# A decoder block's FFN: gate and up computed with the tokens as the stationary operand, their product turned by TensorE transposes, the half-wide block first

## The chip, the core and the metric

The kernel runs on one core of one Trainium2 chip, as one launch. The metric is device microseconds (us) of that core; lower is better. Before the change the median of three runs is 512.78 us.

## What is computed

The block is a pre-norm decoder layer over 256 tokens and a model width of 1024, all in float32. The change touches only its last stage, a SwiGLU FFN with 2816 hidden columns:

```python
h2 = rmsnorm(x, ffn_norm_g[l])
x = x + (jax.nn.silu(h2 @ w_ffn_gate[l]) * (h2 @ w_ffn_up[l])) @ w_ffn_down[l]
```

Ahead of it stand a normalised input projection, two branches (a gated linear recurrence and a block-sparse attention), their gates and the output projection `w_out`; these are as they were.

## The kernel before

All dense products run in split precision. A float32 value is held as a rounded part `hi` (type fp32r) and the rest `lo`; a product is the sum of three, hi·hi, hi·lo and lo·hi. Weights come from HBM in pieces of 1 MB (`load_w`, line 57): one DMA on SyncE's queue into `wraw`, a copy on ScalarE (ACT) that makes `whi` (line 55), and a subtraction on VectorE (DVE) that makes `wlo` (line 56). Each of the three has three buffers, so a piece's buffers are reused three pieces later. Activations that are to be multiplied get the same split.

There are two forms of a dense product. In `tok_block` and in the way down, 128 tokens are the stationary operand (the 128x128 block loaded into TensorE) and 512 weight columns stream past: three matmuls of 512 columns for each 128 inputs and 128 tokens, the result with tokens on the partitions. In `feat_block` (line 86) 128 weight columns are stationary and the tokens stream: for each 128 inputs and 128 outputs one matmul of `whi` against 512 columns (256 tokens hi and 256 tokens lo side by side, line 99) and one of `wlo` against 256 columns (line 98, line 101 for the first of a bank). The result has features on the partitions and its two halves lie side by side, so `fold` (lines 110, 111) adds them with one ACT copy and one DVE add.

The FFN (lines 558 to 634) turns the normalised x2 with TensorE transposes (line 567) into `x2T`, spreads the token scale r2 over the partitions with two small products (`spread`, line 184), and walks over five groups of 512 hidden columns and a last group of 256. In each group `feat_block` makes gate, then up; the folds, the scale, the SiLU and the product give `zt`, already features by tokens, which is what the way down needs as stationary operand. `hT` is its split. `down` (line 584), one group behind, adds two 128-row pieces of `w_down` at a time into four accumulator banks `acc` with matmuls at lines 596 to 598 and at the end adds to x2 and writes out.

Each engine runs its instructions in one fixed order, made at build time by a list scheduler; an instruction that waits holds up all behind it on its engine. PSUM has eight banks: four called `pw` for the products, two `ph` and two `pa` which become `acc` in the FFN.

Of the kernel before, what the change touches and what calls it, by code (L numbers as in the profile page):

```python
# [7 lines left out]
F32 = mybir.dt.float32  # L8
F32R = mybir.dt.float32r
U32 = mybir.dt.uint32  # L10
AF = mybir.ActivationFunctionType
OP = mybir.AluOpType
AX = mybir.AxisListType

P = 128
S = 256
D = 1024
# [3 lines left out]
NFT = DFF // P  # L21
# [6 lines left out]
def tile_hgrn2_moba_block(ctx: ExitStack, tc: tile.TileContext, xm, xT, vecs, table, onehot,  # L28
                          w_in, w_hg, w_at, w_out, w_gate, w_up, w_down, out):
    nc = tc.nc  # L30
    const = ctx.enter_context(tc.tile_pool(name="const", bufs=1))
    big = ctx.enter_context(tc.tile_pool(name="big", bufs=1))
# [5 lines left out]
    def pw(name="pw"):  # L38
        return psum.tile([P, 512], F32, name=name, tag="pw", bufs=4)

    def ph(name="ph"):
        return psum.tile([P, 512], F32, name=name, tag="ph", bufs=2)

    def pa(name="pa"):
        return psum.tile([P, 512], F32, name=name, tag="pa", bufs=2)
# [8 lines left out]
    def split(src, hi, lo):  # L54
        nc.scalar.copy(hi, src)  # L55
        nc.vector.tensor_sub(lo, src, hi.bitcast(F32))  # L56

    def load_w(src, shape, cut=1):
        raw = wp.tile([P] + shape, F32, name="wraw")
        hi = wp.tile([P] + shape, F32R, name="whi")  # L60
        lo = wp.tile([P] + shape, F32R, name="wlo")
        n = shape[0] // cut
        for i in range(0, shape[0], n):
            nc.sync.dma_start(raw[:, i:i + n, :], src[:, i:i + n, :])
            split(raw[:, i:i + n, :], hi[:, i:i + n, :], lo[:, i:i + n, :])
        return hi, lo
# [19 lines left out]
    def feat_block(w, c0, act, cw=512, parts=(4, 4), cut=1):  # L86
        n = cw // P
        ps = [pw() for _ in range(n)]
        k = 0
        for pn in parts:  # L90
            hi, lo = load_w(w[k * P:(k + pn) * P, c0:c0 + cw].rearrange("(k p) c -> p k c", p=P), [pn, cw], cut)
            for ct in range(n):
                cs = slice(ct * P, (ct + 1) * P)
                for i in range(pn):
                    kt = k + i
                    both = act[kt // 4][:, kt % 4, :, :].rearrange("p m t -> p (m t)")
                    if kt > 0:
                        nc.tensor.matmul(ps[ct][:, 0:S], lo[:, i, cs], part(act, kt, 0), start=False, stop=False)  # L98
                    nc.tensor.matmul(ps[ct], hi[:, i, cs], both, start=(kt == 0), stop=(kt == KT - 1))  # L99
                    if kt == 0:  # L100
                        nc.tensor.matmul(ps[ct][:, 0:S], lo[:, i, cs], part(act, kt, 0), start=False, stop=False)  # L101
            k += pn
        return ps

    def fold(dst, p):
        if len(dst.shape) == 3:
            lo, hi = (p[:, m * S:(m + 1) * S].rearrange("p (b t) -> p b t", b=2) for m in range(2))
        else:
            lo, hi = p[:, 0:S], p[:, S:2 * S]
        nc.scalar.copy(dst, hi)  # L110
        nc.vector.tensor_add(dst, lo, dst)  # L111

    def flat():
        return big.tile([P, 4, S], F32, name="fl", tag="T15")
# [14 lines left out]
    for g, pieces in enumerate(((1, 1, 2), (2, 2))):  # L129
# [4 lines left out]
        for n in pieces:  # L134
            ks = slice(k0, k0 + n)
            xs = slice(4 * g + k0, 4 * g + k0 + n)
# [4 lines left out]
            for kt in range(xs.start, xs.stop):  # L141
# [3 lines left out]
                                               op0=OP.mult, op1=OP.subtract)  # L145
                if kt == xs.start:
                    split(raw[:, ks, :], wh[:, ks, :], wl[:, ks, :])
            for i in range(k0, k0 + n):
                kt = 4 * g + i
                for tb in range(2):  # L150
                    ts = slice(tb * P, (tb + 1) * P)
# [7 lines left out]
    ident = const.tile([P, P], F32, name="ident")  # L159
# [3 lines left out]
    for j in range(7):  # L163
        c = 1 << j
        n = 64 // c
        for tb in range(2):
            m = mask[:, j, tb, :].rearrange("p (n c) -> p n c", c=c)
# [11 lines left out]
    def spread(dst, r):  # L179
        dg = small.tile([P, 2, P], F32, name="dg")  # L180
        bank = ph()
        for tb in range(2):
            nc.vector.tensor_scalar_mul(dg[:, tb, :], ident, r[:, tb:tb + 1])
            nc.tensor.matmul(bank[:, tb * P:(tb + 1) * P], ones, dg[:, tb, :], start=True, stop=True)
        nc.vector.tensor_copy(dst, bank[:, :S])
# [369 lines left out]
            split(g, M[half][:, 2 * j:2 * j + 2, 0, :], M[half][:, 2 * j:2 * j + 2, 1, :])  # L555


    x2T = [big.tile([P, 4, 2, S], F32R, name=f"x2T{i}", tag=("XH", "XL")[i]) for i in range(2)]
    ss2 = small.tile([P, 2, 2], F32, name="ss2")
    for half in range(2):  # L560
        ps = tok_block(w_out, half * 512, M)
        for tb in range(2):
            xs = x2[:, tb, half * 512:(half + 1) * 512]
            nc.vector.tensor_add(xs, xs, ps[tb])
            bank = ph()
            for i in range(4):
                nc.tensor.transpose(bank[:, i * P:(i + 1) * P], xs[:, i * P:(i + 1) * P], ident)
            xg = big.tile([P, 4, P], F32, name="xg", tag=("T12", "T13")[tb])
            nc.vector.tensor_mul(xg, bank.rearrange("p (k t) -> p k t", k=4),
                                 vec[:, 8 + half * 4:12 + half * 4].unsqueeze(2).to_broadcast([P, 4, P]))  # L570
            split(xg, x2T[half][:, :, 0, tb * P:(tb + 1) * P], x2T[half][:, :, 1, tb * P:(tb + 1) * P])
            jk2 = big.tile([P, 512], F32, name="jk2", tag="T15")
            nc.scalar.activation(jk2, xs, AF.Square, accum_out=ss2[:, tb, half:half + 1])
    r2 = small.tile([P, 2], F32, name="r2")
    nc.vector.tensor_add(r2, ss2[:, :, 0], ss2[:, :, 1])
    rinv(r2, r2, D)
    R2 = const.tile([P, S], F32, name="R2")
    spread(R2, r2)
    R2b = R2.unsqueeze(1).to_broadcast([P, 2, S])


    acc = [[None, None], [None, None]]

    def down(f0, nf, act, last):
        for j0 in range(0, nf, 2):
            hi, lo = load_w(w_down[(f0 + j0) * P:(f0 + j0 + 2) * P, :].rearrange("(j p) c -> p j c", p=P), [2, D])
            end = last and j0 + 2 == nf
            for tb in range(2):
                for half in range(2):
                    ts = slice(tb * P, (tb + 1) * P)  # L590
                    cs = slice(half * 512, (half + 1) * 512)
                    for i in range(2):
                        j = j0 + i
                        st = f0 + j == 0
                        en = f0 + j == NFT - 1
                        nc.tensor.matmul(acc[tb][half], act[:, j, 0, ts], hi[:, i, cs], start=st, stop=False)  # L596
                        nc.tensor.matmul(acc[tb][half], act[:, j, 0, ts], lo[:, i, cs], start=False, stop=False)  # L597
                        nc.tensor.matmul(acc[tb][half], act[:, j, 1, ts], hi[:, i, cs], start=False, stop=en)  # L598
                    if end:
                        cut = 2 if tb == 1 and half == 1 else 1  # L600
                        cw = 512 // cut
                        for q in range(cut):
                            xs = x2[:, tb, half * 512 + q * cw:half * 512 + (q + 1) * cw]
                            nc.vector.scalar_tensor_tensor(xs, acc[tb][half][:, q * cw:(q + 1) * cw], r2[:, tb:tb + 1],
                                                           xs, op0=OP.mult, op1=OP.add)
                            nc.sync.dma_start(out[tb * P:(tb + 1) * P, half * 512 + q * cw:half * 512 + (q + 1) * cw],
                                              xs)

    pend = None
    for f0 in range(0, NFT, 4):  # L610
        nf = min(4, NFT - f0)
        pg = feat_block(w_gate, f0 * P, x2T, cw=nf * P)
        zt = big.tile([P, 4, S], F32, name="zt", tag=("T12", "T13")[f0 // 4 % 2])
        for j in range(nf // 2):
            z = zt[:, 2 * j:2 * j + 2, :]
            for i in range(2):
                fold(z[:, i, :], pg[2 * j + i])
            nc.vector.tensor_mul(z, z, R2b)
            nc.scalar.activation(z, z, AF.Silu)
        pu = feat_block(w_up, f0 * P, x2T, cw=nf * P)  # L620
        fl = flat()
        hT = big.tile([P, 4, 2, S], F32R, name="hT", tag=("T5", "T6")[f0 // 4 % 2])
        for j in range(nf // 2):
            js = slice(2 * j, 2 * j + 2)
            for i in range(2 * j, 2 * j + 2):
                fold(fl[:, i, :], pu[i])
            nc.vector.tensor_mul(zt[:, js, :], zt[:, js, :], fl[:, js, :])
            split(zt[:, js, :], hT[:, js, 0, :], hT[:, js, 1, :])
        if pend is not None:
            if pend[0] == 0:  # L630
                acc = [[ph("acc00"), ph("acc01")], [pa("acc10"), pa("acc11")]]
            down(*pend, False)
        pend = (f0, nf, hT)
    down(*pend, True)


def _bucket(n):
# [38 lines left out]
```

## Time and profile before

| | us |
|---|---|
| runs | 512.7, 512.78, 514.68; median 512.78 |
| the profiled execution | 513.5 |
| its span, first to last instruction | 511.4 |
| FFN on TensorE, from its first gate matmul to the end of its last matmul's turn | 322.09 to 507.33, that is 185.24 |
| of that: 352 pairs of gate and up matmuls, 264 matmuls of the way down, 8 transposes, 4 records of `spread` | |

The granted TensorE clock is 1.00 of full speed over the whole span (2.4 GHz, the upper of its two levels). A matmul's recorded duration is longer than the time until the next one starts, since they are pipelined; time from start to start is what a chain costs.

### The profile page before, as it was taken

The numbers are of one execution on the slowest core, as the hardware profiler recorded it, in microseconds if no ns is written. First come the engines' busy times: TensorE is split into PE (matmuls) and PEld (weight loads), VectorE is DVE, ScalarE is ACT, GpSimd is POOL, SyncE is SP. The second block draws the span as 40 slices with busy tenths as digits, with TensorE's granted clock in tenths as the row PEclk, the third lists the DMA queues.
The fourth block names the chain that finished last, engine by engine and source line by source line (L and its number), as shares of the span: only waits on it lengthen the run. The fifth ranks groups of instructions, "written<-read, shape, count | busy, mean of one in ns | idle before, by whom it ended". The sixth has DMA issues, their size and how long they took to land.

```text
span 511.4 us, 6690 instructions
## 1 busy us (share of the span) xinstructions
PE 502.2 (98%) x2674; PEld 427.5 (84%) x2674; DVE 350.9 (69%) x406; ACT 291.8 (57%) x447; POOL 25.4 (5%) x42
## 2 busy tenths in 40 slices
PE   6999999999999999999999999999999999999996
PEld 5878878788888888988888888888888888888885
DVE  4769998977597663297667777767665646657372
ACT  5597538776639644975554464665634535444250
POOL 8002340000000000000000000000000000000000
PEclk9999999999999999999999999999999999999999
DMA  7956955725422743256665456555655565553522
GB/s 234 390 197 182 347 178 168 243 82 166 164 84 82 247 142 106 83 171 242 190 213 173 166 181 229 165 164 172 208 198 164 186 226 165 177 193 86 181 105 82
DMA packets 43806, 91.20 MB, mean 178 GB/s; under 512 B 1880, under 2 KB 4472, under 8 KB 43776
## 3 DMA queue, kind: packets, MB, share of 16 engines
q1 hardware_dynamic: 43040, 88.14, 51.8%
q0 software_dynamic: 736, 2.65, 1.7%
q8 instruction: 21, 0.34, 0.3%
q14 instruction: 9, 0.07, 0.0%
HBM read 89.70 MB, written 1.07 MB: 178 GB/s over the span
## 4 chain that ended last, share of the span: by engine, by line
PE 86%; DVE 6%; ACT 3%; DMA 1%; POOL 1%; issue 1%; SPq 0%; DVEq 0%; POOLq 0%
PE pw L99 30%; PE pw L98 13%; PE pw L83 6%; PE pw L81 6%; PE pw L82 6%; PE acc L598 4%; PE acc L596 4%; PE acc L597 4%; DVE wlo L56 3%; PE ph L320 2%; PE pw L101 2%; ACT whi L55 2%; DMA wraw<-w_in 1%; POOL qk L295 1%; PE pa L437 1%
## 5 line engine op out<-in xcount | busy, mean ns | idle before, releaser
L56 DVE TENSOR_TENSOR wlo<-wraw,whi 128x2048 fp32r<-128x2048 f32 (+2 forms) x88 | 190.8, 2169 | 105.4 <-ACT whi L55 105.0
L55 ACT CAST whi<-wraw 128x2048 fp32r<-128x2048 f32 (+2 forms) x88 | 156.0, 1774 | 104.4 <-issue 29.5
L99 PE MATMUL pw<-x2T,whi 128*128 128x512 f32 x352 | 121.8, 398 | 0.0
L99 PE MATMUL pw<-XT,whi 128*128 128x512 f32 x256 | 89.6, 399 | 0.0
L98 PE MATMUL pw<-x2T,wlo 128*128 128x256 f32 x308 | 86.6, 281 | 0.0
L99 PEld LDWEIGHTS pw<-x2T,whi 128*128 128x128 f32 x352 | 63.5, 188 | 12.3
L98 PE MATMUL pw<-XT,wlo 128*128 128x256 f32 x224 | 62.8, 281 | 0.0
L98 PEld LDWEIGHTS pw<-x2T,wlo 128*128 128x128 f32 x308 | 58.3, 189 | 1.8
L81 PE MATMUL pw<-whi,XT 128*128 128x512 f32 x144 | 56.9, 395 | 0.8 <-DVE Q L111 0.8
L82 PE MATMUL pw<-wlo,XT 128*128 128x512 f32 x144 | 56.8, 394 | 0.0
L83 PE MATMUL pw<-whi,XT 128*128 128x512 f32 x144 | 56.5, 392 | 0.0
L99 PEld LDWEIGHTS pw<-XT,whi 128*128 128x128 f32 x256 | 46.5, 188 | 9.9 <-ACT Fg L110 0.4
L98 PEld LDWEIGHTS pw<-XT,wlo 128*128 128x128 f32 x224 | 42.4, 189 | 1.4
L596 PE MATMUL acc<-whi,hT 128*128 128x512 f32 x88 | 34.3, 390 | 0.0
L598 PE MATMUL acc<-whi,hT 128*128 128x512 f32 x88 | 34.3, 390 | 0.0
L597 PE MATMUL acc<-wlo,hT 128*128 128x512 f32 x88 | 34.3, 389 | 0.0
L81 PEld LDWEIGHTS pw<-whi,XT 128*128 128x128 f32 x144 | 27.1, 188 | 6.5 <-DVE Q L111 1.1
L83 PEld LDWEIGHTS pw<-whi,XT 128*128 128x128 f32 x144 | 27.0, 188 | 5.6
L82 PEld LDWEIGHTS pw<-wlo,XT 128*128 128x128 f32 x144 | 27.1, 188 | 5.5 <-DVE wlo L56 0.3
L110 ACT COPY fl<-pw 128x256 f32<-128x256 f32 x38 | 14.0, 370 | 24.9 <-PE pw L99 24.9
L99 PE MATMUL pw<-aT,whi 128*128 128x512 f32 x64 | 22.3, 397 | 0.0
L99 PE MATMUL pw<-oT,whi 128*128 128x512 f32 x64 | 22.3, 397 | 0.0
(209 smaller groups left out, 708.4 us busy)
## 6 DMA issues: line engine op xcount, KB each, us to landing
wraw<-w_in SPq DMA_DIRECT2D x32, 1024.0 KB, 5.2
wraw<-w_down SPq DMA_DIRECT2D x11, 1024.0 KB, 4.8
wraw<-w_gate SPq DMA_DIRECT2D x10, 1024.0 KB, 5.0
wraw<-w_up SPq DMA_DIRECT2D x10, 1024.0 KB, 5.0
wraw<-w_at SPq DMA_DIRECT2D x4, 1024.0 KB, 4.9
wraw<-w_hg SPq DMA_DIRECT2D x4, 1024.0 KB, 5.0
wraw<-w_out SPq DMA_DIRECT2D x4, 1024.0 KB, 5.0
wraw<-w_in SPq DMA_DIRECT2D x7, 512.0 KB, 8.8
```

The source lines that it names most:

```text
L55: nc.scalar.copy(hi, src)
L56: nc.vector.tensor_sub(lo, src, hi.bitcast(F32))
L81: nc.tensor.matmul(ps[tb], part(act, kt, 0)[:, ts], wh, start=(kt == 0), stop=False)
L82: nc.tensor.matmul(ps[tb], part(act, kt, 0)[:, ts], wl, start=False, stop=False)
L83: nc.tensor.matmul(ps[tb], part(act, kt, 1)[:, ts], wh, start=False, stop=(kt == KT - 1))
L98: nc.tensor.matmul(ps[ct][:, 0:S], lo[:, i, cs], part(act, kt, 0), start=False, stop=False)
L99: nc.tensor.matmul(ps[ct], hi[:, i, cs], both, start=(kt == 0), stop=(kt == KT - 1))
L101: nc.tensor.matmul(ps[ct][:, 0:S], lo[:, i, cs], part(act, kt, 0), start=False, stop=False)
L110: nc.scalar.copy(dst, hi)
L596: nc.tensor.matmul(acc[tb][half], act[:, j, 0, ts], hi[:, i, cs], start=st, stop=False)
L597: nc.tensor.matmul(acc[tb][half], act[:, j, 0, ts], lo[:, i, cs], start=False, stop=False)
L598: nc.tensor.matmul(acc[tb][half], act[:, j, 1, ts], hi[:, i, cs], start=False, stop=en)
```

## The change

Gate and up are computed in the token form: tokens stationary, 512 weight columns streaming (256 in the half-wide group, which now goes first). `x2T` is stored by 128 tokens (`cb`). The SiLU on ACT reads a bank directly and takes r2 as its per-partition scale, so `fold`, `spread` and the multiplication with R2 are gone; a DVE multiplication with the up bank, also read directly, gives `zt`, tokens by features. For the way down `turn` transposes `zt` on TensorE, a group later, into the banks that up will use next (`bX`, `bZ`), and `split` reads them there and writes `hT`. The way down takes its pieces from a list, `todo`, at fixed places between the gate and up blocks. `pw`'s four banks get fixed roles: `bV`, `bY` gate for the two token halves, `bX`, `bZ` up.

```diff
-    x2T = [big.tile([P, 4, 2, S], F32R, name=f"x2T{i}", tag=("XH", "XL")[i]) for i in range(2)]
+    xq = big.tile([P, 2, 2, 4, P], F32, name="xq", tag="T11")
+    cb = []
+    for tag in ("XH", "XL"):
+        two = big.tile([P, 2, 4, 2, P], F32R, name="cb" + tag, tag=tag)
+        cb += [two[:, 0], two[:, 1]]
+
+    def combine(m, p):
+        split(xq[:, p[0], p[1]], cb[m][:, :, 0, :], cb[m][:, :, 1, :])
...
-    R2 = const.tile([P, S], F32, name="R2")
-    spread(R2, r2)
-    R2b = R2.unsqueeze(1).to_broadcast([P, 2, S])
...
+    acc = [[ph("acc00"), ph("acc01")], [pa("acc10"), pa("acc11")]]
+    bV, bY, bX, bZ = pw("bV"), pw("bY"), pw("bX"), pw("bZ")
+
+    def product(ps, c, hi, lo, first, last):
+        for k in range(4):
+            nc.tensor.matmul(ps, c[:, k, 0, :], hi[:, k, :], start=(first and k == 0), stop=False)
+            nc.tensor.matmul(ps, c[:, k, 0, :], lo[:, k, :], start=False, stop=False)
+            nc.tensor.matmul(ps, c[:, k, 1, :], hi[:, k, :], start=False, stop=(last and k == 3))
...
+        def gate(self, tb, src):
+            nc.scalar.activation(self.z[:, tb], src, AF.Silu, scale=r2[:, tb:tb + 1])
+
+        def turn(self, tb, bank):
+            for j in range(self.nf):
+                nc.tensor.transpose(bank[:, j * P:(j + 1) * P], self.z[:, tb, j * P:(j + 1) * P], ident)
+            src = bank[:, :self.cw].rearrange("p (j t) -> p j t", j=self.nf)
+            ts = slice(tb * P, (tb + 1) * P)
+            split(src, self.hT[:, :self.nf, 0, ts], self.hT[:, :self.nf, 1, ts])
+            if tb == 1:
+                todo.extend((self.hT, self.f, j0) for j0 in range(0, self.nf, 2))
...
+        def block(self, w, banks, kh):
+            hi, lo = load_w(self.quarter(w, kh), [4, self.cw])
             for tb in range(2):
+                product(banks[tb][:, :self.cw], cb[plain[kh][tb]], hi, lo, kh == 0, kh == 1)
+
+        def run(self, prev):
+            self.open()
+            self.block(w_gate, (bV, bY), 0)
+            if prev:
+                down()
+            else:
+                self.block(w_up, (bX, bZ), 0)
+            self.block(w_gate, (bV, bY), 1)
+            for tb in range(2):
+                self.gate(tb, (bV, bY)[tb][:, :self.cw])
+            if prev:
+                prev.turn(0, bX)
+                prev.turn(1, bZ)
+                self.block(w_up, (bX, bZ), 0)
+                down()
+            self.block(w_up, (bX, bZ), 1)
+            self.close()
+            for tb in range(2):
+                nc.vector.tensor_mul(self.z[:, tb], self.z[:, tb], (bX, bZ)[tb][:, :self.cw])
+
+    order = ((5, Eight), (0, Eight), (1, Eight), (2, Eight), (3, Eight), (4, Eight))
...
-        pg = feat_block(w_gate, f0 * P, x2T, cw=nf * P)
...
-            for i in range(2):
-                fold(z[:, i, :], pg[2 * j + i])
-            nc.vector.tensor_mul(z, z, R2b)
-            nc.scalar.activation(z, z, AF.Silu)
-        pu = feat_block(w_up, f0 * P, x2T, cw=nf * P)
...
-            nc.vector.tensor_mul(zt[:, js, :], zt[:, js, :], fl[:, js, :])
-            split(zt[:, js, :], hT[:, js, 0, :], hT[:, js, 1, :])
+    down()
+    prev.turn(0, bV)
+    prev.turn(1, bY)
+    while todo:
+        down()
```

TensorE in the changed kernel, at the place where the fourth group's gate ends (`whi_3240` is its gate piece, `zt_3010` the third group's product, `whi_3314` and `wlo_3315` a piece of `w_down`, `whi_3284` a piece of up):

```order
L596 MATMUL bY_2717<-whi_3240,cbXL_2537 128x512
L645 MATMUL bX_2718<-ident_185,zt_3010 128x128 x4
L645 MATMUL bZ_2719<-ident_185,zt_3010 128x128 x4
L613 MATMUL acc00_2712<-whi_3314,hT_3175 128x512
L614 MATMUL acc00_2712<-wlo_3315,hT_3175 128x512
L613 MATMUL acc01_2713<-whi_3314,hT_3175 128x512
L614 MATMUL acc01_2713<-wlo_3315,hT_3175 128x512
L594 MATMUL bX_2718<-whi_3284,cbXH_2536 128x512
```

Eight transposes and the way down's first four matmuls now stand between gate and up; those four read `hT_3175`, which is made from the transposes just ahead of them. In the kernel before, the same engine passes from the third group's up to the way down of the group ahead of it (`hT_3086`), made during the block in between:

```order
L98 MATMUL pw_3261<-x2T1_2536,wlo_3302 128x256
L99 MATMUL pw_3261<-x2T1_2536,whi_3301 128x512
L596 MATMUL acc00_3101<-whi_3355,hT_3086 128x512
L597 MATMUL acc00_3101<-wlo_3356,hT_3086 128x512
L598 MATMUL acc00_3101<-whi_3355,hT_3086 128x512
```

ACT in the changed kernel at the same place (`bV` and `bY` are the fourth group's gate, `hT_3175` the hi part of the turned product):

```order
L55 CAST whi_3314<-wraw_3313 128x2048
L641 ACTIVATE zt_3178<-bV_2716,r2_2707 128x512
L641 ACTIVATE zt_3178<-bY_2717,r2_2707 128x512
L55 CAST hT_3175<-bX_2718 128x4x128
L55 CAST hT_3175<-bZ_2719 128x4x128
L55 CAST whi_3344<-wraw_3343 128x2048
```

The SiLU of both gate banks stands ahead of the copies that TensorE's next matmul reads. In the kernel before, ACT's order around a group's product is this (`fl_3085` up's fold, `hT_3086` its split):

```order
L110 COPY fl_3085<-pw_3008 128x256
L55 CAST whi_3170<-wraw_3169 128x2048
L55 CAST hT_3086<-zt_2992 128x2x256 x2
L55 CAST whi_3208<-wraw_3207 128x2048
```

There the copy into `hT` has a whole block of other matmuls ahead of its reader.

## Rows read from the trace of the kernel before

**Rows 1.** Page, first part: engine, busy us, share of the span, instructions.

```profile
PE 502.2 (98%) x2674; PEld 427.5 (84%) x2674; DVE 350.9 (69%) x406; ACT 291.8 (57%) x447; POOL 25.4 (5%) x42
```

**Rows 2.** TensorE's waits over the whole span: us in total, times, longest.

```profile
PE pw L152 <- ACT whi L55: 2.8, 2, 2.4
...
PE ph L305 <- DVE A L306: 0.2, 1, 0.2
```

**Rows 3.** Busy time by stretch: us, PE, PEld, DVE, ACT, POOL, clock, DMA share, GB/s.

```profile
368.49:379.39 10.90, 10.90 (x49) 9.01 (x48) 7.33 (x7) 5.13 (x5) 0.00 (x0) 1.00 0.58 194
379.39:401.92 22.53, 22.53 (x129) 19.61 (x128) 13.04 (x14) 10.98 (x13) 0.00 (x0) 1.00 0.57 188
490.96:507.33 16.37, 16.37 (x73) 13.34 (x71) 8.16 (x9) 2.81 (x3) 0.00 (x0) 1.00 0.09 33
...
322.09:368.49 46.40, 46.40 (x269) 40.41 (x268) 33.43 (x44) 28.43 (x38) 0.00 (x0) 1.00 0.54 182
```

**Rows 4.** Timeline of TensorE from the way down into gate: start, us, operation.

```profile
378.94 0.39 PE L597 MATMUL acc<-wlo,hT 128*128 128x512 f32 x1
379.17 0.39 PE L598 MATMUL acc<-whi,hT 128*128 128x512 f32 x1
379.39 0.39 PE L99 MATMUL pw<-x2T,whi 128*128 128x512 f32 x1
379.62 0.28 PE L101 MATMUL pw<-x2T,wlo 128*128 128x256 f32 x1
379.73 0.28 PE L98 MATMUL pw<-x2T,wlo 128*128 128x256 f32 x1
379.85 0.40 PE L99 MATMUL pw<-x2T,whi 128*128 128x512 f32 x1
380.08 0.28 PE L98 MATMUL pw<-x2T,wlo 128*128 128x256 f32 x1
```

**Rows 5.** Timeline of TensorE at the FFN's start, four transposes among matmuls.

```profile
322.09 0.39 PE L99 MATMUL pw<-x2T,whi 128*128 128x512 f32 x1
322.36 0.66 PE L567 MATMUL ph<-ident,x 128*128 128x128 f32 x4
322.77 0.36 PE L101 MATMUL pw<-x2T,wlo 128*128 128x256 f32 x1
322.97 0.28 PE L98 MATMUL pw<-x2T,wlo 128*128 128x256 f32 x1
```

**Rows 6.** The transposes of line 567: recorded duration in ns, min/median/max.

```profile
L567 PE MATMUL ph<-ident,x x16: 272/273/328, 310.5 to 323.4; 128*128 128x128 f32 x16
```

**Rows 7.** Timeline of TensorE, a chain of short matmuls in the recurrence.

```profile
153.50 1.95 PE L320 MATMUL ph<-QA,KP 128*128 128x128 f32 x16
155.19 0.48 PE L81 MATMUL pw<-whi,XT 128*128 128x512 f32 x1
```

**Rows 8.** Timeline, a 256-column matmul whose stationary operand came late.

```profile
31.78 2.29 DVE L56 TENSOR_TENSOR wlo<-wraw,whi 128x2048 fp32r<-128x2048 f32 x1 [1.05 <-ACT whi L55]
...
34.13 0.39 PE L101 MATMUL pw<-XT,wlo 128*128 128x256 f32 x1
...
34.35 0.28 PE L98 MATMUL pw<-XT,wlo 128*128 128x256 f32 x1
```

**Rows 9.** Timeline from TensorE over ACT to DVE, attention's values and the SiLU ahead.

```profile
180.91 0.39 PE L83 MATMUL pw<-whi,XT 128*128 128x512 f32 x1
...
181.33 1.37 ACT L509 ACTIVATE sg<-pw,rx 128x512 f32<-128x512 f32 x2 [1.55 <-PE pw L83]
...
183.32 0.58 ACT L55 CAST aT<-pa 128x512 fp32r<-128x512 f32 x1 [0.62 <-PE pa L474]
...
183.94 0.69 DVE L56 TENSOR_TENSOR aT<-pa,aT 128x512 fp32r<-128x512 f32 x1 [3.13 <-ACT aT L55]
```

**Rows 10.** Timeline of ACT, two scaled copies out of PSUM back to back.

```profile
153.07 1.31 ACT L221 ACTIVATE Va<-pw,rx 128x512 f32<-128x512 f32 x2 [0.71 <-PE pw L83]
```

**Rows 11.** The fold copy of line 110, 256 columns out of PSUM: duration in ns.

```profile
L110 ACT COPY zt<-pw x22: 358/372/374, 330.7 to 485.5; 128x256 f32<-128x256 f32 x22
```

**Rows 12.** The SiLU of line 509, read from PSUM: duration in ns.

```profile
L509 ACT ACTIVATE sg<-pw,rx x4: 687/688/688, 181.3 to 200.0; 128x512 f32<-128x512 f32 x4
```

More of the change, by code (lines that the diff above doesn't have):

```diff
@@ L555, in tile_hgrn2_moba_block @@
             split(g, M[half][:, 2 * j:2 * j + 2, 0, :], M[half][:, 2 * j:2 * j + 2, 1, :])
-    x2T = [big.tile([P, 4, 2, S], F32R, name=f"x2T{i}", tag=("XH", "XL")[i]) for i in range(2)]
+    xq = big.tile([P, 2, 2, 4, P], F32, name="xq", tag="T11")
[5 more added lines that the diff above has]
+        split(xq[:, p[0], p[1]], cb[m][:, :, 0, :], cb[m][:, :, 1, :])
+    plain = [[0, 1], [2, 3]]
     ss2 = small.tile([P, 2, 2], F32, name="ss2")
@@ L567, in tile_hgrn2_moba_block @@
                 nc.tensor.transpose(bank[:, i * P:(i + 1) * P], xs[:, i * P:(i + 1) * P], ident)
-            xg = big.tile([P, 4, P], F32, name="xg", tag=("T12", "T13")[tb])
-            nc.vector.tensor_mul(xg, bank.rearrange("p (k t) -> p k t", k=4),
+            nc.vector.tensor_mul(xq[:, half, tb], bank.rearrange("p (k t) -> p k t", k=4),
                                  vec[:, 8 + half * 4:12 + half * 4].unsqueeze(2).to_broadcast([P, 4, P]))
-            split(xg, x2T[half][:, :, 0, tb * P:(tb + 1) * P], x2T[half][:, :, 1, tb * P:(tb + 1) * P])
+            combine(plain[half][tb], (half, tb))
             jk2 = big.tile([P, 512], F32, name="jk2", tag="T15")
@@ L576, in tile_hgrn2_moba_block @@
     rinv(r2, r2, D)
-    R2 = const.tile([P, S], F32, name="R2")
-    spread(R2, r2)
-    R2b = R2.unsqueeze(1).to_broadcast([P, 2, S])
[L582 to L587, printed above, removed]
-            for tb in range(2):
-                for half in range(2):
-                    ts = slice(tb * P, (tb + 1) * P)
-                    cs = slice(half * 512, (half + 1) * 512)
-                    for i in range(2):
[L593 to L607, printed above, removed]
@@ L609, in tile_hgrn2_moba_block @@
-    pend = None
-    for f0 in range(0, NFT, 4):
-        nf = min(4, NFT - f0)
-        pg = feat_block(w_gate, f0 * P, x2T, cw=nf * P)
[L613 to L616, printed above, removed]
-                fold(z[:, i, :], pg[2 * j + i])
-            nc.vector.tensor_mul(z, z, R2b)
-            nc.scalar.activation(z, z, AF.Silu)
-        pu = feat_block(w_up, f0 * P, x2T, cw=nf * P)
[L621 to L626, printed above, removed]
-            nc.vector.tensor_mul(zt[:, js, :], zt[:, js, :], fl[:, js, :])
-            split(zt[:, js, :], hT[:, js, 0, :], hT[:, js, 1, :])
[L629 to L633, printed above, removed]
@@ L634, in tile_hgrn2_moba_block @@
-    down(*pend, True)
+    acc = [[ph("acc00"), ph("acc01")], [pa("acc10"), pa("acc11")]]
+    bV, bY, bX, bZ = pw("bV"), pw("bY"), pw("bX"), pw("bZ")
+    todo = []
+    done = [0]
+    def product(ps, c, hi, lo, first, last):
[3 more added lines that the diff above has]
+            nc.tensor.matmul(ps, c[:, k, 1, :], hi[:, k, :], start=False, stop=(last and k == 3))
@@ new lines, in down @@
+    def down():
+        if not todo:
+            return
+        hT, f, j0 = todo.pop(0)
+        hi, lo = load_w(w_down[(f + j0) * P:(f + j0 + 2) * P, :].rearrange("(j p) c -> p j c", p=P), [2, D])
+        done[0] += 2
+        for tb in range(2):
+            for half in range(2):
+                ts = slice(tb * P, (tb + 1) * P)
+                cs = slice(half * 512, (half + 1) * 512)
+                ac = acc[tb][half]
+                for i in range(2):
+                    j = j0 + i
+                    st = done[0] == 2 and i == 0
+                    en = done[0] == NFT and i == 1
+                    nc.tensor.matmul(ac, hT[:, j, 0, ts], hi[:, i, cs], start=st, stop=False)
+                    nc.tensor.matmul(ac, hT[:, j, 0, ts], lo[:, i, cs], start=False, stop=False)
+                    nc.tensor.matmul(ac, hT[:, j, 1, ts], hi[:, i, cs], start=False, stop=en)
+                if done[0] == NFT:
+                    cut = 2 if tb == 1 and half == 1 else 1
+                    cw = 512 // cut
+                    for q in range(cut):
+                        os = slice(half * 512 + q * cw, half * 512 + (q + 1) * cw)
+                        nc.vector.scalar_tensor_tensor(x2[:, tb, os], ac[:, q * cw:(q + 1) * cw], r2[:, tb:tb + 1],
+                                                       x2[:, tb, os], op0=OP.mult, op1=OP.add)
+                        nc.sync.dma_start(out[ts, os], x2[:, tb, os])
@@ new lines, in tile_hgrn2_moba_block, with __init__, quarter, open @@
+    class Unit:
+        def __init__(self, n, u):
+            self.n, self.f, self.c0 = n, 4 * u, u * 512
+            self.nf = min(4, NFT - 4 * u)
+            self.cw = self.nf * P
+        def quarter(self, w, r):
+            return w[r * 512:(r + 1) * 512, self.c0:self.c0 + self.cw].rearrange("(k p) c -> p k c", p=P)
+        def open(self):
+            self.z = big.tile([P, 2, 512], F32, name="zt", tag=("T12", "T13")[self.n % 2])[:, :, :self.cw]
+        def close(self):
+            self.hT = big.tile([P, 4, 2, S], F32R, name="hT", tag=("T6", "T8")[self.n % 2])
+        def gate(self, tb, src):
[4 more added lines that the diff above has]
+            src = bank[:, :self.cw].rearrange("p (j t) -> p j t", j=self.nf)
+            ts = slice(tb * P, (tb + 1) * P)
+            split(src, self.hT[:, :self.nf, 0, ts], self.hT[:, :self.nf, 1, ts])
+            if tb == 1:
+                todo.extend((self.hT, self.f, j0) for j0 in range(0, self.nf, 2))
@@ new lines, in tile_hgrn2_moba_block @@
+    class Eight(Unit):
+        def block(self, w, banks, kh):
+            hi, lo = load_w(self.quarter(w, kh), [4, self.cw])
+            for tb in range(2):
+                product(banks[tb][:, :self.cw], cb[plain[kh][tb]], hi, lo, kh == 0, kh == 1)
[16 more added lines that the diff above has]
+            self.close()
+            for tb in range(2):
+                nc.vector.tensor_mul(self.z[:, tb], self.z[:, tb], (bX, bZ)[tb][:, :self.cw])
@@ L637, in _bucket @@
+    order = ((5, Eight), (0, Eight), (1, Eight), (2, Eight), (3, Eight), (4, Eight))
+    units = [kind(n, u) for n, (u, kind) in enumerate(order)]
+    prev = None
+    for n, one in enumerate(units):
+        one.run(prev)
+        prev = one
+    down()
[3 more added lines that the diff above has]
+        down()
 def _bucket(n):
```

## The prediction

> **What bounds the kernel now.** I read the page's first part, then TensorE's waits, then the busy times by stretch, then the timeline of single matmuls. TensorE is busy 98% of the span [rows 1], and none of its four waits, of which the longest and the shortest are shown, is on a line of the FFN [rows 2]. So the FFN, 322.09 to 507.33, is a gapless chain of TensorE work, and its price is the time from each start to the next. Recorded durations mislead here: a 512-column matmul of gate reads 0.40 us and a 256-column one 0.28, together 0.68, but the next pair begins 0.35 later [rows 4]. Grouped: 64 pairs of gate and up take 22.53, or 0.352 a pair; 48 matmuls of the way down take 10.90 and the last 72 take 16.37, or 0.227 each [rows 3]. The first stretch agrees: 46.40 less two groups of 22.53 leaves 1.34 for its eight transposes and four records of `spread` [rows 3]. DVE and ACT are far from full (13.04 and 10.98 of 22.53), DMA is busy a little over half, and the granted clock is 1.00 [rows 3]. Work taken off DVE and ACT is therefore worth nothing by itself; only TensorE's count and its waits matter.
>
> **Gate and up.** Before, 352 pairs at 0.352 are 123.9 us. After, five full groups have 2 weights x 8 input tiles x 2 token halves x 3 products = 96 matmuls of 512 columns each, 480 in all. The trace has this very form in the way down, at 0.227: 109.0. The half-wide group has 96 matmuls of 256 columns. A chain of these alone is not in the trace. The nearest row is two in a row, 0.11 and 0.12 from start to start [rows 4]. Below it stands a chain of shorter ones, sixteen in 1.69, or 0.106 [rows 7]; above it a 256-column matmul whose weight load nothing covers, 0.22 [rows 8]. I take 0.12, the second of the two in a row: 11.5, with 0.106 to 0.13 (10.2 to 12.5) for the range. Sum 120.5, a gain of **3.4**. Read by durations the same edit would seem to gain 25 us (352 x 0.68 against 480 x 0.39 and 96 x 0.28); by columns it gains none, since 512 + 256 for each 128x128 block of weights before are 6 x 512 / 4 = 768 now, and what is left is the small loss at each change between long and short matmuls.
>
> **Transposes.** 22 feature tiles x 2 token halves = 44. Four of them push the next matmul from 322.32 (322.09 plus the 0.23 of the 512-column matmul ahead) to 322.77, that is 0.11 each, and the matmul behind them takes 0.20 instead of 0.11 [rows 5]. 44 x 0.11 and six groups x 0.09 make **+5.4**.
>
> **Spread.** Its four records go, a third of the 1.34 above: **-0.45**.
>
> **Folds, R2, flat buffers.** These are DVE and ACT work under TensorE's cover; nothing, as long as the new ACT and DVE work is covered too. A full group has six pieces to split, two SiLUs, two casts, two subtractions and two products: about 14 us of ACT and 17 of DVE in some 34 us of TensorE. The pieces come at one per 5.45 us against 5.6 before, so the DMA rate hardly changes. A piece's `whi` can be written once the piece three back is done, which leaves two pieces, some 11 us, for a split of about 4. At the FFN's start, gate's second half needs the second half of x2 no earlier than before: 48 short matmuls (5.8) stand where 16 pairs (5.6) stood.
>
> **The new wait.** In the order of the changed kernel, the way down's first four matmuls stand right behind the eight transposes, and the first reads the hi part of what was just turned. So TensorE waits for ACT, and all of up's first half is queued behind it. The chain, from the start of the first transpose: `bY`'s last matmul started 0.23 earlier, and ACT reads a bank 0.42 after its last matmul's start (180.91 to 181.33 [rows 9]), so the second SiLU starts at 0.19. Such an operation reads 0.69 [rows 12], and the next one on ACT may start 0.62 behind it (two in 1.31 [rows 10]), so the cast of `bX` starts at 0.81 and, at the 0.58 of the cast of `aT` [rows 9], ends at 1.39. TensorE starts 0.06 after its releaser ends (31.78 + 2.29 to 34.13 [rows 8]): 1.45. Without the wait it would go on at 8 x 0.11 = 0.88. That is 0.57 for each of four full turns, 2.3. The half-wide group's turn has only four transposes (0.44) and a 256-column cast of 0.37 [rows 11]: 0.81 + 0.37 + 0.06 less 0.44 is 0.80. The last turn has no SiLU ahead: the fourth transpose starts at 0.33, reads 0.27 [rows 6], the cast ends near 1.24, TensorE goes on at 1.30: 0.4. Together **+3.5**. What is late next is up's first matmul, which needs DVE's subtraction of `bX`: 1.39 + 0.04 + 0.69 [rows 9] + 0.06 = 2.18, while the four matmuls put in front end at 1.45 + 0.91 = 2.36. It is covered, by 0.2 only. Bounds: nothing if something else delays TensorE by as much, and 5.5 if each turn costs 0.9 (a cast of 0.69 like the SiLU, and 0.2 of missed cover behind it).
>
> **Sum.** -3.4 + 5.4 - 0.45 + 3.5 = **+5.05** us. The profiled execution took 513.5 (span 511.4 and 2.1 around it), 0.7 above the median of 512.78; on it the sum is 518.55, on the median **517.8**, which I predict.
>
> **Rivals.** *The turn's wait doesn't show* (the cast is done when TensorE arrives, or transposes run slow enough to cover it): +1.55, 514.3, which is inside the 0.5%, about 2.6 us, that a measurement of this kernel can tell from no change. For it speaks that the scheduler chose these four matmuls as cover and that the kernel before has no such wait; against it that ACT's order is fixed with both SiLUs ahead. Chance 0.17.
>
> *TensorE is bound by loading the stationary operand, not by streaming.* Loading is busy 84% [rows 1], and the FFN would have 892 loads for 980 (the 980 are 704, 264, 8 and 4). At their recorded 0.188 (9.01 over 48 [rows 3]) 88 fewer are 16.5 us: 512.8 - 16.5 + 3.5 = 499.8, faster. It decides from the point where a load takes longer than the columns it hides behind. The Trainium skill, "Perfetto Trace Analysis", section "Identifying the Most-Contended Engine", says that matmul busy time is a bad measure of how near the roofline TensorE is, and that the busy share of weight loads is a good one; by that rule this would be the forecast. Against it: a pair with two loads takes 0.352, under twice 0.188, and a chain of loads runs at 0.106 [rows 7], so loads overlap too; and a 512-column matmul with one load takes 0.227. Chance 0.04.
>
> *A transpose holds TensorE for its recorded 0.27 [rows 6]*, not 0.11: 44 x 0.16 = 7.0 more, 524.8. "TensorE: Matmul & The Clock Gate" of the Trainium skill, section "Part 4: PE-mode transpose", gives about 275 ns for a 128x128 one in a kernel; that rule speaks against this change. The duration agrees with the row, but four in a row start 0.11 apart [rows 5]. Chance 0.05.
>
> *The half-wide group's loads are exposed*, 0.22 for each of its 96 matmuls: 9.6 more, 527.4. Against it stand the two in a row. Chance 0.04.
>
> **How the numbers follow.** The forecast, transposes above the gain and a wait at each turn, has 0.70, of which 0.03 lies under 515.3 with short waits. Faster by over 0.5%: 0.04. Within 0.5%: 0.17 + 0.03 = 0.20. Slower: 0.67 + 0.05 + 0.04 = 0.76. The range takes in the first rival and the bounds of the unknown prices: down to 514.3 less half of the 1.3 that 0.106 would give, 513.7; up to 517.8 with 2.0 for longer waits and half of 1.0 for 0.13, 520.3. The three rivals left out hold 0.13.
>
> **What would show it.** In the profile after: gate matmuls of 512 columns 0.227 apart; the half-wide group's 96 in about 11.5; eight transposes in 0.9 with about 0.6 more until the way down's first matmul; on ACT silu, silu, cast, cast without a gap; no other TensorE wait in the FFN. The prediction is wrong if the way down's first matmul follows the transposes at once, if up's first matmul waits as well, if 512-column matmuls run closer than 0.227 with weights streaming, or if the clock falls below 1.00 at the turns.

## The result and the profile after

The changed kernel took 517.95 us in the median of four runs (517.37 to 519.07), the kernel before 513.11 beside it. The ratio is 1.0091, with a 95% interval of 1.0062 to 1.0121: slower, by 4.8 us, where 5.05 was predicted. The profiled execution took 517.5 with a span of 515.4, 4.0 above before; in the FFN alone it is 190.17 against 185.24, or 4.93. The 0.9 between the two lies ahead of the change: the FFN's first matmul starts at 321.19 instead of 322.09. In this kernel and its variants below it starts anywhere between 321.2 and 323.6, so this start is read as no part of the effect.

The page's first part, to be read beside [rows 1]: the busy time of DVE falls by 22.7, of ACT by 13.1 and of the weight loads (PEld) by 2.7, that of TensorE and POOL rises by 1.5 and 1.0, the instructions fall from 6690 to 6423, and the time rises.

```profile
PE 503.7 (98%) x2586; PEld 424.8 (82%) x2586; DVE 328.2 (64%) x350; ACT 278.7 (54%) x405; POOL 26.4 (5%) x42
```

TensorE's three largest waits (us in total, times, longest): a line of the FFN has joined those of [rows 2], six times.

```profile
PE pw L152 <- ACT whi L55: 3.1, 3, 1.7
PE acc L613 <- ACT hT L55: 2.4, 6, 0.6
PE warm L122 <- DVE ones L117: 1.1, 1, 1.1
```

Busy time by stretch, with the columns of [rows 3]: the half-wide group with the eight transposes of x2 among its 96 matmuls, then the second group's gate (48 matmuls of 512 columns), then the whole FFN.

```profile
321.19:333.66 12.47, 12.47 (x105) 12.40 (x104) 8.86 (x13) 11.19 (x15) 0.00 (x0) 1.00 0.68 223
333.66:344.58 10.92, 10.92 (x51) 8.98 (x50) 7.12 (x4) 4.80 (x4) 0.00 (x0) 1.00 0.79 282
321.19:511.36 190.17, 187.80 (x893) 156.56 (x891) 93.75 (x69) 78.77 (x66) 0.00 (x0) 1.00 0.51 172
```

10.92 over 48 is 0.228, nearly the 0.227 of the way down before. 12.47 less 0.95 for the x2 transposes and the two matmuls they delay is 11.5 for 96, as predicted; inside the group such matmuls start 0.120 apart. The granted clock stays at 1.00, the upper level, through all turns.

One turn, the third group's (the second of full width), in the timeline (start, us, engine, operation, and in brackets the idle time ahead and its releaser):

```profile
407.10 0.39 PE L596 MATMUL bY<-whi,cbXL 128*128 128x512 f32 x1
...
407.33 0.60 PE L645 MATMUL bX<-ident,zt 128*128 128x128 f32 x4
407.53 0.69 ACT L641 ACTIVATE zt<-bY,r 128x512 f32<-128x512 f32 x1 [2.03 <-PE bY L596]
...
407.76 0.60 PE L645 MATMUL bZ<-ident,zt 128*128 128x128 f32 x4
408.11 0.58 ACT L55 CAST hT<-bX 128x512 fp32r<-128x512 f32 x1
408.58 0.60 ACT L55 CAST hT<-bZ 128x512 fp32r<-128x512 f32 x1
408.73 0.69 DVE L56 TENSOR_TENSOR hT<-bX,hT 128x512 fp32r<-128x512 f32 x1 [2.40 <-ACT hT L55]
...
408.74 0.50 PE L613 MATMUL acc<-whi,hT 128*128 128x512 f32 x1 [0.38 <-ACT hT L55]
...
409.54 0.40 PE L614 MATMUL acc<-wlo,hT 128*128 128x512 f32 x1
409.78 0.39 PE L594 MATMUL bX<-whi,cbXH 128*128 128x512 f32 x1
```

This is the chain of the prediction nearly to the figure: SiLU 0.20 after the first transpose (0.19 predicted), cast at 0.78 (0.81), the way down at 1.41 (1.45). TensorE's next matmul could have followed at 0.79, so the wait is 0.62 although the bracket says 0.38: the profile counts idle time only from the modelled end of the last transpose, which is 0.24 after the next matmul could have started. Up's first matmul, at 409.78, follows without a wait of its own: DVE was done with `bX` at 409.42, so the cover was 0.3 where 0.2 was predicted.

### The profile page after: what moved, and what is told of

It reads as the page before. It is cut to its first block, busy times and chain, and to the rows that moved or that the text cites. A ratio compares the mean times of both kernels' runs of the same rounds, so it can differ in the third digit from the quotient of the medians.

```text
span 515.4 us, 6423 instructions
## 1 busy us (share of the span) xinstructions
PE 503.7 (98%) x2586; PEld 424.8 (82%) x2586; DVE 328.2 (64%) x350; ACT 278.7 (54%) x405; POOL 26.4 (5%) x42
## 4 chain that ended last, share of the span: by engine, by line
PE 85%; DVE 6%; ACT 4%; issue 1%; POOL 1%; DMA 1%; SPq 0%; DVEq 0%; ACTq 0%; POOLq 0%
PE pw L99 14%; PE pw L83 6%; PE pw L81 6%; PE pw L82 6%; PE pw L98 6%; PE acc L613 4%; PE acc L614 4%; PE acc L615 4%; DVE wlo L56 3%; PE ph L320 2%; PE bY L596 2%; PE bX L596 2%; PE bX L595 2%; PE bX L594 2%; PE bV L594 2%; PE bZ L596 2%
## 5 line engine op out<-in xcount | busy, mean ns | idle before, releaser
L613 PEld LDWEIGHTS acc<-whi,hT 128*128 128x128 f32 x88 | 16.5, 188 | 7.0 <-ACT hT L55 3.8
L615 PEld LDWEIGHTS acc<-whi,hT 128*128 128x128 f32 x88 | 16.5, 188 | 3.5
L614 PEld LDWEIGHTS acc<-wlo,hT 128*128 128x128 f32 x88 | 16.5, 188 | 3.2
L322 DVE COPY_PREDICATED A<-mask,ph 128x512 f32<-128x512 uint32 x14 | 12.4, 891 | 10.3 <-PE ph L320 10.3
L98 PE MATMUL pw<-aT,wlo 128*128 128x256 f32 x56 | 15.7, 281 | 0.0
```

The lines of the kernel that those rows point to most:

```text
L613: nc.tensor.matmul(ac, hT[:, j, 0, ts], hi[:, i, cs], start=st, stop=False)
L614: nc.tensor.matmul(ac, hT[:, j, 0, ts], lo[:, i, cs], start=False, stop=False)
L615: nc.tensor.matmul(ac, hT[:, j, 1, ts], hi[:, i, cs], start=False, stop=en)
```

## The experiments

**The transposes one block earlier.** If the wait is ACT's chain, work between turn and reader removes it.

```diff
...
             if prev:
-                down()
+                old = len(todo)
+                prev.turn(0, bX)
+                prev.turn(1, bZ)
+                if old:
+                    down()
...
-            if prev:
-                prev.turn(0, bX)
-                prev.turn(1, bZ)
                 self.block(w_up, (bX, bZ), 0)
...
```

> The changed kernel with each group's transposes moved one block earlier: behind the first gate block of the next group instead of behind the second, so that a gate block or a piece of the way down (5.4 us) stands between the transposes and the first matmul that reads hT; the last turn goes between the two token halves of a piece of the way down. Counts of instructions are the same. Theory (the six waits of 0.39 to 0.76 us, 3.3 us in all, are TensorE waiting for ACT's SiLU, SiLU, cast chain): 3.3 us faster than the changed kernel, about +1.5 us on the kernel before, and no wait on the way down's first matmul. Rival (the pause behind eight transposes is a cost of TensorE's own at a change from transposes to matmuls): as slow as the changed kernel, +4.8 us, with the pause now behind the transposes at their new place.

Measured: 514.12 us, ratio 1.001 to the kernel before (0.9998 to 1.0022). The FFN is a gapless chain of 186.10, which is 4.07 less than the changed kernel's and 0.86 more than before. The timeline of TensorE at the new place:

```profile
396.53 0.39 PE L596 MATMUL bY<-whi,cbXH 128*128 128x512 f32 x1
396.76 0.60 PE L647 MATMUL bX<-ident,zt 128*128 128x128 f32 x4
397.19 0.60 PE L647 MATMUL bZ<-ident,zt 128*128 128x128 f32 x4
397.55 0.48 PE L615 MATMUL acc<-whi,hT 128*128 128x512 f32 x1
397.87 0.40 PE L616 MATMUL acc<-wlo,hT 128*128 128x512 f32 x1
```

The stretch of the whole FFN in this run, with the columns of [rows 3]:

```profile
323.03:509.13 186.10, 186.10 (x893) 156.39 (x891) 93.32 (x69) 78.82 (x66) 0.00 (x0) 1.00 0.53 176
```

The next matmul starts 0.79 after the first of eight transposes, and the one behind it follows after 0.32 instead of 0.23. So there is no pause of TensorE's own behind transposes, and the wait was worth 4.07 rather than 3.3. The early turn is level with the kernel before within the interval, not 1.5 above it.

**The same without transposes.** `turn` splits `zt` as it stands, out of SBUF and not out of a bank, so the way down multiplies features and tokens in the wrong places; nothing else in the code differs from the early turn.

```diff
-            for j in range(self.nf):
-                nc.tensor.transpose(bank[:, j * P:(j + 1) * P], self.z[:, tb, j * P:(j + 1) * P], ident)
-            src = bank[:, :self.cw].rearrange("p (j t) -> p j t", j=self.nf)
+            src = self.z[:, tb].rearrange("p (j t) -> p j t", j=self.nf)
```

> The same, and the 44 transposes left out: hT is split straight from zt, untransposed, so the way down multiplies the wrong features and tokens; all else is as it was. It measures the token form of gate and up by itself, with no turn and no wait. Theory: 44 x 0.11 and six changes of 0.1 less, 5.4 us faster than the early turn, which is 3.9 us faster than the kernel before (3.4 from the matmuls, 0.45 from the spread). Rival (gate and up gain nothing in this form, and the loss of the change lies in them): no faster than the kernel before.

Measured: 509.29 us, ratio 0.991 (0.9891 to 0.9929). The stretch of its whole FFN, with the columns of [rows 3]:

```profile
323.60:504.74 181.14, 181.14 (x849) 151.86 (x847) 93.24 (x69) 79.53 (x66) 0.00 (x0) 1.00 0.54 181
```

181.14 is 4.96 less than with the transposes in the early place, 0.113 for each of 44, and 4.10 less than before. Gate and up do gain in the token form (with the spread gone), and the transposes alone give it all back.

**All transposes twice.** This was to show that a longer row of transposes hides in ACT's chain.

```diff
-            for j in range(self.nf):
+            for j in list(range(self.nf)) * 2:
                 nc.tensor.transpose(bank[:, j * P:(j + 1) * P], self.z[:, tb, j * P:(j + 1) * P], ident)
```

> The changed kernel with every transpose issued twice into the same place, 44 more, at the old place. Theory: 44 x 0.109 = 4.8 us more of transposes, but sixteen of them last 1.74 us, as long as ACT's chain (first cast done near 1.7), so that of the 3.3 us of waits only some 0.4 at the half-wide group stay: +1.9 us on the changed kernel. Rival (the wait is not that chain, or starts only when the transposes end): +4.8 us or more. If a transpose held TensorE for its recorded 0.27 us: +12 us.

Measured: 528.4 us, ratio 1.0276 (1.0258 to 1.0293), some 9.5 above the changed kernel. The theory's 1.9 fails; the rival's "4.8 or more" takes it in, but for another reason, which the timeline of a full turn shows:

```profile
410.37 1.03 PE L645 MATMUL bX<-ident,zt 128*128 128x128 f32 x8
410.57 0.69 ACT L641 ACTIVATE zt<-bY,r 128x512 f32<-128x512 f32 x1 [2.03 <-PE bY L596]
...
411.16 1.90 ACT L55 CAST whi<-wraw 128x2048 fp32r<-128x2048 f32 x1
411.24 1.04 PE L645 MATMUL bZ<-ident,zt 128*128 128x128 f32 x8
412.95 0.59 ACT L55 CAST hT<-bX 128x512 fp32r<-128x512 f32 x1
...
413.59 0.50 PE L613 MATMUL acc<-whi,hT 128*128 128x512 f32 x1 [1.31 <-ACT hT L55]
```

With the transposes ending later, the scheduler put the split of a weight piece (1.90) between the SiLU and the cast. The cast starts 2.58 after the first transpose instead of 0.78, and TensorE's matmul starts 0.64 after the cast's start, nearly as in the changed kernel (408.11 to 408.74). At the full turns the run doesn't test what it was meant to, but it shows the chain once more, 1.8 us longer: TensorE's start moves with ACT's order one for one. At the half-wide turn nothing slid in, and there eight transposes for four leave the way down's start where it was, 1.20 after the first transpose for 1.21. Up's first matmul waits as well in this run:

```profile
PE bX L594 <- DVE hT L56: 1.3, 4, 0.3
```

On DVE, too, the subtraction of a weight piece (2.29, from 413.08) stands ahead of that of `bX`. This is the wait that the prediction counted among the signs that it is wrong; the changed kernel itself doesn't have it.

**Half the transposes twice.** The same question with the second token half alone doubled; here the scheduler keeps SiLU, SiLU and first cast together.

```diff
-            for j in range(self.nf):
+            for j in list(range(self.nf)) * (1 + tb):
                 nc.tensor.transpose(bank[:, j * P:(j + 1) * P], self.z[:, tb, j * P:(j + 1) * P], ident)
```

> The changed kernel with the transposes of the second token half alone issued twice, 22 more; ACT copies the first half's turn right behind the two SiLUs, as in the changed kernel, and only then splits a weight piece. Theory (TensorE waits 0.62 us at a full turn for ACT's SiLU, SiLU, cast, which doesn't get longer): the four transposes added at each turn, 0.43 us, fill the wait and cost nothing: no difference from the changed kernel within 0.5 us. Rival (the pause is TensorE's own and stays): 22 x 0.109 = +2.4 us.

Measured: 518.45 us, ratio 1.009 (1.0061 to 1.0119), the changed kernel's ratio. The timeline:

```profile
408.86 0.60 PE L645 MATMUL bX<-ident,zt 128*128 128x128 f32 x4
409.06 0.69 ACT L641 ACTIVATE zt<-bY,r 128x512 f32<-128x512 f32 x1 [2.03 <-PE bY L596]
409.29 1.04 PE L645 MATMUL bZ<-ident,zt 128*128 128x128 f32 x8
409.64 0.58 ACT L55 CAST hT<-bX 128x512 fp32r<-128x512 f32 x1
...
410.27 0.50 PE L613 MATMUL acc<-whi,hT 128*128 128x512 f32 x1
```

Twelve transposes or eight, the way down starts 1.41 after the first. The four added ones are free, and the bracket for the wait is gone at this turn though 0.2 of it is still there. The stretch of the whole FFN, with the columns of [rows 3]:

```profile
322.65:513.08 190.43, 190.04 (x915) 158.56 (x913) 93.85 (x69) 78.86 (x66) 0.00 (x0) 1.00 0.51 172
```

That is 0.26 above the changed kernel's 190.17, where 22 transposes in the open would have added 2.4. Together with the early turn this settles that the lost time at a turn is ACT's chain.

**The half-wide group last.**

```diff
-    order = ((5, Eight), (0, Eight), (1, Eight), (2, Eight), (3, Eight), (4, Eight))
+    order = ((0, Eight), (1, Eight), (2, Eight), (3, Eight), (4, Eight), (5, Eight))
```

> The changed kernel with the half-wide group last instead of first, the one part of the change that is an order. Theory: the group's 96 short matmuls and its turn cost the same wherever they stand. Five full turns wait 0.62 us each and the last, half-wide one some 0.5, 3.6 us for 3.8: no difference from the changed kernel within 0.5 us. Rival (the half-wide group stands first because the start needs small pieces): TensorE waits at the FFN's start for the first full piece or for the second half of x2, 1 to 3 us slower.

Measured: 519.77 us, ratio 1.0119 (1.0091 to 1.0146), which overlaps the changed kernel's. The FFN takes 190.73, 0.56 more. TensorE has no wait at the FFN's start, so the rival falls. What is longer is the fifth turn, on the timeline:

```profile
488.28 0.60 PE L645 MATMUL bX<-ident,zt 128*128 128x128 f32 x4
488.48 0.47 ACT L641 ACTIVATE zt<-bY,r 128x256 f32<-128x256 f32 x1 [0.60 <-PE bY L596]
...
488.85 1.03 ACT L55 CAST whi<-wraw 128x1024 fp32r<-128x1024 f32 x1
489.79 0.59 ACT L55 CAST hT<-bX 128x512 fp32r<-128x512 f32 x1
...
490.43 0.50 PE L613 MATMUL acc<-whi,hT 128*128 128x512 f32 x1 [1.11 <-ACT hT L55]
```

Again a weight split, here a half-wide one of 1.03, stands ahead of the cast, and the way down starts 2.15 after the first transpose, 0.74 later than at the other full turns. The order of the groups by itself is worth nothing that these runs can tell.

**A chain of 128-column matmuls.** 96 of them, with changing stationary operands, ahead of the second group's second gate block. This is for the rival that the load bounds TensorE.

```diff
+            if self.n == 1 and w is w_gate and kh == 1:
+                for i in range(96):
+                    nc.tensor.matmul(bX[:, :P], cb[i // 4 % 2][:, i % 4, 0, :], hi[:, i % 4, :P], start=True, stop=True)
```

> The changed kernel with 96 matmuls of 128 columns added ahead of the second group's second gate block, each with another stationary operand than the one before it, into a bank that nothing reads before it is written anew. It measures where the load of the stationary operand takes over from the streamed columns. The half-wide group's chains run at 120.0 ns and the full ones at 226.7, which is 256 and 512 columns at 2.4 GHz plus 13.4 ns both times. If the columns still decide at 128, the chain runs at 53.3 + 13.4 = 67 ns and costs 6.4 us. If the load decides, it runs at the 0.106 to 0.112 us of the trace's other short chains, and costs 10 to 11 us.

Measured: 529.26 us, ratio 1.0305 (1.0274 to 1.0337), some 11 above the changed kernel. The stretch of the added chain, with the columns of [rows 3]:

```profile
339.86:350.53 10.67, 10.67 (x98) 10.67 (x96) 2.29 (x1) 1.91 (x1) 0.00 (x0) 1.00 0.74 270
```

10.67 is 0.111 for each; with columns alone deciding, the expectation's estimate was 6.4 in all. So something else decides at 128 columns. The load, one for each matmul, is the likely cause, but no run changed the load alone, so another floor for short matmuls isn't ruled out. Either way a load needs at most 0.111 from start to start, not its recorded 0.188. The 256-column matmuls of the half-wide group, at 0.120, stand just above that, and 512-column ones far above: the loader rival would need narrower matmuls than those of this FFN.

**Long and short matmuls in pairs.** In the kernel before, `feat_block` alternates a 512- and a 256-column matmul. Swapping every second pair puts two of a kind together.

```diff
-                    if kt > 0:
+                    if kt % 2 == 1:
                         nc.tensor.matmul(ps[ct][:, 0:S], lo[:, i, cs], part(act, kt, 0), start=False, stop=False)
                     nc.tensor.matmul(ps[ct], hi[:, i, cs], both, start=(kt == 0), stop=(kt == KT - 1))
-                    if kt == 0:
+                    if kt % 2 == 0:
                         nc.tensor.matmul(ps[ct][:, 0:S], lo[:, i, cs], part(act, kt, 0), start=False, stop=False)
```

> The kernel before with the two matmuls of every second pair in feat_block swapped, so that two 512-column matmuls stand together and then two 256-column ones, in all 736 pairs of the kernel. It asks where the 3.4 us that the token form gains come from. Theory (each change between a long and a short matmul costs some ns, since the weights of the long one load under the short one): the few such groups in the trace of before take 0.696 us for two pairs against 0.704, so 736 x 0.004 = 2.8 us faster than the kernel before. Rival (the price is the short matmul's own, however it is placed): no difference.

Measured: 511.83 us, ratio 0.9959 (0.9943 to 0.9976). It beats both kernels. The stretch of one group of 64 pairs, to be read beside 22.53 in [rows 3]:

```profile
379.36:401.65 22.29, 22.29 (x129) 19.45 (x128) 12.97 (x14) 10.99 (x13) 0.00 (x0) 1.00 0.57 189
```

That is 0.3483 a pair for 0.352, or 2.8 us over 736 pairs; the ratio shows 2.1 (its interval reaches from 1.2 to 2.9).

**In fours.** Four long, four short, then in a block's second half four short, four long.

```diff
-                for i in range(pn):
-                    kt = k + i
...
+                for m in ((0, 1) if k == 0 else (1, 0)):
+                    for i in range(pn):
+                        kt = k + i
...
```

> The kernel before with feat_block's matmuls sorted into fours: four of 512 columns, then four of 256, and the other way round in the second half of a block. It asks the same as the pairs with half as many changes between long and short. Pairs took 0.3482 us for a long and a short one where alternating took 0.352; both lengths in chains of their own take 0.2267 + 0.1200 = 0.3467. Theory (the loss sits at the changes): about 0.3475, so 736 x 0.0045 = 3.3 us faster than the kernel before, 0.5 faster than pairs. Rival (the loss is something else that pairs happened to avoid): no faster than pairs.

Measured: 515.3 us, ratio 1.0042 (1.0022 to 1.0063): slower than before where the theory gave 3.3 faster; the rival, no faster than pairs, is right, but doesn't say why it is slower. One of its twelve executions, the profiled one, took 1769.25 us and is no part of the ratio; the profile below is from a further run.

> The kernel of the fours once more, for a profile alone: it was 1.6 us slower than the kernel before where 3.3 faster was expected, and its profiled execution had TensorE nearly four times slower throughout, so that nothing can be read from it. If the loss sits at the changes between long and short matmuls, the FFN's groups of 64 pairs take 64 x 0.3475 = 22.24 us here (22.29 in pairs, 22.53 alternating) and the loss is a wait elsewhere, most likely at the first pieces, which come in two DMAs and whose four long matmuls now all stand ahead of the short ones. If not, the groups themselves take 22.6 us or more.

Measured: 515.38 us in one run. The stretch of a group of 64 pairs, with the columns of [rows 3]:

```profile
381.81:404.23 22.42, 22.42 (x129) 19.61 (x128) 13.43 (x14) 11.09 (x13) 0.00 (x0) 1.00 0.59 191
```

The longest of TensorE's waits in the same run (us in total, times, longest):

```profile
PE pw L81 <- DVE Q L111: 3.0, 1, 3.0
```

The same wait in the kernel before:

```profile
PE pw L81 <- DVE Q L111: 0.8, 1, 0.8
```

The groups take 0.3503 a pair, between alternating and pairs, so the loss doesn't shrink with the number of changes, and that explanation falls. In this execution the FFN takes 184.72, 0.52 less than before, and starts 2.52 later; one wait ahead of it, for DVE's fold of Q, grew by 2.2 and accounts for most of that. Why it grew is open. Why pairs lose least is open too: in the mean of these stretches a long matmul takes 0.235 alternating, 0.233 in pairs and 0.232 in fours, for 0.227 in a chain of its own, and a short one 0.117, 0.115 and 0.118, for 0.120. Pairs are ahead of fours at the short matmuls alone.

## Why the prediction was right

The two experiments without wait and without turn split the FFN's 4.93 into the prediction's own steps:

| step | predicted | measured | from |
|---|---|---|---|
| gate, up and the spread | -3.85 | -4.10 | no transposes against before |
| 44 transposes | +5.4 | +4.96 | early turn against no transposes |
| the wait at six turns | +3.5 | +4.07 | changed kernel against early turn |
| sum | +5.05 | +4.93 | |

*Gate and up.* Right, since start to start was used and not durations; the matmuls ran at the 0.227 and 0.120 that it took. The gain was 0.25 larger than forecast.

*Transposes.* A little high. Eight in a row with one delayed matmul cost 0.88 (0.79, and 0.09 on the matmul behind) and not 0.97: the prediction put the 0.09 on top of eight full steps of 0.11, while the next matmul already starts at 0.79.

*The wait.* The chain was right link by link; a turn's wait is 0.62 against 0.57, since TensorE could have gone on at 0.79 and not 0.88. That is the same error as in the transposes, with the other sign, and the two nearly cancel. Half-wide and last turn came to 0.85 and 0.48 (0.80 and 0.4). The six waits add up to 3.81; most of what is left of the 4.07 lies in the matmuls right behind them, whose first four take 1.04 at a full turn (408.74 to 409.78) and 1.01 in the early place; the last 0.1 isn't assigned. Up's first matmul didn't wait, as predicted. The prediction's upper bound for the wait, 5.5, is 5.4 by its own terms, which changes nothing here.

*How close.* That the total is met within 0.2 is in part luck. The steps are off by -0.25, -0.44 and +0.57, of which the last two belong together and the first happens to help, and the interval of the ratio reaches from 3.2 to 6.2 us.

*The rivals.* The wait that doesn't show is what the early turn makes. There the rival's sum of +1.55 was too high: the FFN is 0.86 longer than before. The loader rival is out: the FFN's loads fell from 980 to 892, their busy share of the span from 84% to 82%, and time rose. The Trainium skill's rule that the busy share of loads, beside the share of peak arithmetic, tells how near TensorE is to its roofline ("Perfetto Trace Analysis", section "Identifying the Most-Contended Engine") would have misled here. Recorded loads of 0.188 overlap and can follow each other at 0.111. The transposes' recorded 0.27 isn't what they cost either: they cost 0.113 each. The figure of about 275 ns in the Trainium skill's "TensorE: Matmul & The Clock Gate", section "Part 4: PE-mode transpose", agrees with the recorded duration and not with the cost. The half-wide group's loads were not exposed: its matmuls start 0.120 apart, not 0.22.

## What to carry to other kernels

Where one engine is full, count what stays on it, from start to start: here a form that streams the same columns saved a little per matmul, and the transposes it needs cost more. The 22.7 us of DVE and 13.1 of ACT that disappeared bought no time that these runs show, since TensorE waited for neither in the FFN before. A new product that is turned, copied and read at once is a chain that it does wait for, so put the turn a block ahead of its reader: here that took back 4.07 us, and left the change level with the kernel before. When an experiment changes timing under a scheduler, compare the orders of all engines first: twice here a weight split slid into the chain.

## What the runs showed of the hardware

- With a new stationary operand each, fp32r matmuls in a chain start 0.2267 apart at 512 columns and 0.1200 at 256, at a granted clock of 1.00; both are 13.4 ns above the columns at 2.4 GHz, the upper level. At 128 columns it is 0.111, and not the 0.067 that the same sum would give; that the load of the stationary operand decides there is likely and not shown.
- Transposes of 128x128 float32 start 0.109 apart in a row, at a granted clock of 1.00, for a recorded 0.27. Right behind eight of them the next matmul starts 0.79 after the first.
- The idle time in the profile's brackets understates a wait of TensorE, since a matmul's modelled end lies later than the point where the next could start: 0.38 was shown for 0.62, and nothing for 0.2.
- A 512-column matmul behind 256-column ones takes 0.23 to 0.24 instead of 0.227, and sorting into pairs (0.3483 for a long and a short one) saves more than sorting into fours (0.3503). What causes it stays open.
